# All 22 tiles of gate and up as seven products, with the first two products of 16 tiles computed early and kept in DRAM

## The chip, the cores and the metric

The kernel runs on one core of a Trainium2 chip. The time is that of the device for one execution, in microseconds. Before the change it is 1148.82 us, the median of three runs (1148.8 to 1149.24). The engines are named as in the profile: PE is TensorE, DVE is VectorE, ACT is ScalarE, POOL is GpSimd, SP is SyncE, which issues most DMAs.

## The reference, cut to what matters

One decoder layer on a sequence of 1024 rows of 1024 floats: a norm, attention over windows and a state-space scan in parallel, an output projection, a second norm, and a gated feed-forward network of width 2816. The change touches the part from the scan on.

```python
x = x + gate1 * hybrid_mixer(h, ...)              # attention and scan, then @ w_o
h = rmsnorm(x, norm2) * (1.0 + scale2) + shift2   # the second norm
gu = h @ w_gate_up                                # 1024 x 1024 by 1024 x 5632
g, u = gu[..., :D_FF], gu[..., D_FF:]
x = x + gate2 * ((silu(g) * u) @ w_down)
```

All of it is float32 in and out. Each float32 operand is split into a high and a low part, and a product is three matmuls (`mm3`, L93: high by high, high by low, low by high).

## The kernel before

Gate and up have 22 tiles (`NF`) of 128 columns each. The 1024 rows are two halves of 512, and the 1024 inner rows are eight k-tiles of 128. `h2[half][kt]` is the result of the second norm, transposed and split.

A tile can be done in two ways. In the plain one (`gate_up`, L725), gate and up of one half are eight k-steps of `mm3` each: 48 matmuls for a half, 96 for both. In the other one (`gate_up7`, L881), a two-by-two block scheme after Winograd treats gate and up, the two halves of the inner rows and the two halves of the sequence as blocks, and needs seven products of four k-steps instead of eight: 84 matmuls. The products take sums of the weights' blocks (`w_operand`, L856: four sums on DVE, and for each product a split, which is a cast on ACT and a subtraction on DVE) and sums of h2's blocks (`h2_sums`, L839). Product 0 is the upper half of the gate's weights by the first four k-tiles of h2 of the first half, product 1 the lower half by the last four; their sum is the gate of the first half. Products 2, 3, 4 and 6 take the sums of h2, product 5 takes h2 of the second half, and they need both halves.

Tiles 0 to 3 (`early = 4`) are done the plain way. Their first halves fill PE while the scan's last four chunks (`ssd_chunk`, L573) and the second half's norm wait for other engines; their second halves follow the second half's norm, and cover the time in which the sums of h2 are made. Tiles 4 to 21 are done in seven products. After every pair of tiles `act_sums` (L818) makes four sums on POOL for the seven products of the down projection, and stores seven blocks to DRAM; `dn_weight` (L806) does the like for a block of w_down, in 11 of the tiles (from tile 9 on).

The program is written in one order; a planner lists the instructions of each engine from it, by their order in the program and the time at which it reckons them ready, so instructions of later lines stand between earlier ones. Each engine runs its own list in order. DMAs of SP (`dma`, L71) keep the program's order: SP is a queue in which each DMA waits for the one ahead. ACT issues a few DMAs itself.

Memory: raw weights pass through a ring of three slots (`raw_ring`), split ones through `ws_ring` and, for the seven products, `w_ring` of ten slots. PSUM has four banks tagged "mm" and four tagged "sm". The pools FA and FB hold everything up to the second norm; after it they are closed (L785), and GR and GF are opened in the same memory. `store` (L743) notes a store to DRAM, and `flush` (L746) issues those noted.

Of the kernel before, what the change touches and what calls it, by code (L numbers as in the profile page):

```python
# [15 lines left out]
P = 128  # L16
D = 1024
KT = 8
NF = 22
XNB = ((0, 4, 36, 40), (0, 4, 36, 40))  # L20
# [12 lines left out]
FP_MISC = 1536  # L33
FR_N, FP_N, FA_N, FB_N = 109 * 256, FP_MISC + 3072, 70 * 256 + 8, 6480
GR_N, GF_N, GD_N = 44 * 256, 50 * 256, 92 * 256
# [3 lines left out]
def hymba_layer(ctx: ExitStack, tc: tile.TileContext, x, ada01, ada_rest, w_qk, w_vz, w_xbc,  # L39
# [662 lines left out]
    def second_norm(half, xr, ss):  # L702
        xn = []
        for t in range(4):
            s1 = ring([1], "ss1", 4)
            add(s1, ss[t][:, 0:1], ss[t][:, 1:2])
            r = rstd_of(s1, D, f"r2_{half}{t}", 1)
            n = xn_buf[half][t]
            for e in range(2):
                es = slice(512 * e, 512 * e + 512)  # L710
                nc.vector.tensor_scalar(out=n[:, es], in0=xr[t][:, es], scalar1=r, scalar2=None, op0=ALU.mult)
            dma(x1_d[4 * half + t], xr[t])
            xn.append(n)
        hf_ring = Ring([(FA, 66.03125), (FA, 68.03125)] + ([(FA, 10), (FA, 12)], [(FA, 32), (FA, 34)])[half])
        for kt in range(KT):
            hf = hf_ring([512])
            h_tile(h2[half][kt], xn, kt, g2, sh2, hf, f"h2{half}_{kt}", sm_bank, nc.vector.tensor_copy)
            nc.scalar.dma_start(h2_d[half][kt], hf)
# [4 lines left out]
    early = 4  # L723

    def gate_up(f, half, out, then=None):  # L725
        pss = []
        for s in range(2):
            if (f, s) not in resident:
                resident[(f, s)] = load_w(w_gu[f + NF * s], [KT, P])
            h, l = resident[(f, s)]  # L730
            ps = mm_bank(f"psgu{f}{s}{half}")
            for kt in range(KT):
                t = h2[half][kt]
                mm3(ps, h[:, kt], l[:, kt], t[:, 0], t[:, 1], kt == 0, kt == KT - 1)
            pss.append(ps)
            if then:
                then(s)
        nc.scalar.activation(out, pss[0], AF.Silu)
        mul(out, out, pss[1])
# [41 lines left out]
    for _ in range(3):  # L781
        fetch()
    second_norm(1, xr, ss)
    flush()
# [5 lines left out]
    u_ring, c11, u4 = ring_at(GF, 6, 2, 2), view(GF, 10, [512]), view(GF, 12, [512])  # L790
    pair_ring = ring_at(GF, 14, 8, 2)
    s_act = [view(GF, 30 + 2 * k, [512]) for k in range(3)]
    w_pair = view(GF, 36, [4, 512])
    t_pair = [view(GF, 44 + 2 * k, [512]) for k in range(3)]
# [23 lines left out]
    def act_sums(i, a):  # L818
# [6 lines left out]
        for j, v in (("a11", a11), ("a12", a12), ("a22", a22), ("s1", s1), ("s2", s2), ("s3", a21), ("s4", s4)):  # L825
            if 2 * i >= early or j not in ("a11", "a12"):
                store(act_d, j, i, v)
# [5 lines left out]
    h2_set = [[view(GF, kb + 2 * k, [512]) for k in range(6)] for kb in (36, 0)]  # L833
# [11 lines left out]
    resident = dict(pre)  # L845

    def early_load(n):
        if n < len(order):
            hl = ws_ring([2, D])
            h, l = (hl[:, j].rearrange("p (a b) -> p a b", a=KT) for j in range(2))  # L850
            split(h, l, fetched.pop(order[n]))
            resident[order[n]] = h, l
            fetch()


    def w_operand(n):  # L856
        f, j = divmod(n, 7)
        f += early
        if f >= NF:
            return  # L860
        g, u = fetched[f, 0], fetched[f, 1]
        a11, a12, a21, a22 = g[:, 0:4], g[:, 4:8], u[:, 0:4], u[:, 4:8]
        if j == 2:
            add(s1_w, a21, a22)
            sub(s2_w, s1_w, a11)
        elif j == 4:
            sub(s3_w, a11, a21)
        elif j == 5:
            sub(s2_w, a12, s2_w)
        v = (a11, a12, s2_w, s1_w, s3_w, s2_w, a22)[j]  # L870
        w = w_ring([2, 4, P])
        split(w[:, 0], w[:, 1], v)
        w_ops[n] = w
        if j > 4:
            fetch()

    w_ops = {}
    AHEAD = 5
    rhs = (h2[0][0:4], h2[0][4:8], op_t2, op_t1, op_t3, h2[1][4:8], op_t4)

    def gate_up7(f, out0, out1):  # L881
        u = u_ring([512])
        for j in range(7):
            n = 7 * (f - early) + j
            w_operand(n + AHEAD)
            w, ps = w_ops.pop(n), (mm_bank, sm_bank)[n % 2](f"psg7_{j}_{f}")
# [269 lines left out]
```

## Time and profile before

| | before |
|---|---|
| median of three runs | 1148.82 us |
| profiled execution | 1144.76 us, span 1143.0 us |
| PE, PEld busy | 97%, 80% |
| DVE, ACT, POOL busy | 74%, 45%, 21% |
| mean granted clock of PE | 0.987 |
| DMA | 197.29 MB, 173 GB/s over the span |

The profile is of one execution. Times in it count from the start of its span; the execution takes 1.76 us more than the span. Busy PE counts the time in which a matmul is anywhere in the pipeline, and matmuls overlap, so the pace is read from the starts of many. A bracket behind a row of the timeline is idle time of the engine ahead of that instruction, and what ended it.

### The profile page before, as it was taken

Reading aid. Unit: us, or ns where it says so; the run is one execution under the profiler, and the core shown is the slowest. Engines: PE = TensorE matmul, PEld = TensorE weight load, DVE = VectorE, ACT = ScalarE, POOL = GpSimd, SP = SyncE. Lnnn points to the kernel's source line nnn. Section 1 sums busy time; section 2 is a strip of 40 time slices with the busy share of each in tenths; the row PEclk is TensorE's granted clock in tenths of the full one; section 3 lists DMA queues with packets and bytes.
Section 4 is the critical chain, followed back from the end, with each engine's and each line's share of the span. In section 5 each row is a group of like instructions: output and inputs, shape, how many; then the busy total and the mean of one; then the engine's idle time right before and its main releaser. Section 6 shows DMA issues by size and latency. Waiting matters only on the chain. (4 is left out here: it accounts for less than half of the span.)

```text
span 1143.0 us, 15497 instructions
## 1 busy us (share of the span) xinstructions
PE 1105.0 (97%) x5376; PEld 912.4 (80%) x5376; DVE 842.6 (74%) x1490; ACT 517.2 (45%) x1007; POOL 244.6 (21%) x185
## 2 busy tenths in 40 slices
PE   7999999999999889999999999999999999999996
PEld 6788987787788668887888888888888878888875
DVE  6895368788856466546888888898788648787856
ACT  4573256756565456535443333333333325555431
POOL 0100000001200111000222124554445010451352
PEclk9999999999999969999999999999999999999998
DMA  7555644421320253236753247556764468788733
GB/s 267 189 173 174 238 151 145 137 74 38 148 75 19 102 185 119 76 127 221 249 189 125 67 148 263 194 179 217 256 201 160 157 226 306 252 292 281 234 104 147
DMA packets 80449, 197.29 MB, mean 173 GB/s; under 512 B 9154, under 2 KB 10226, under 8 KB 80244
## 3 DMA queue, kind: packets, MB, share of 16 engines
q1 hardware_dynamic: 74164, 184.95, 47.4%
q10 hardware_dynamic: 6208, 11.37, 2.8%
q8 instruction: 42, 0.69, 0.2%
q14 instruction: 35, 0.29, 0.1%
HBM read 149.87 MB, written 47.98 MB: 173 GB/s over the span
## 5 line engine op out<-in xcount | busy, mean ns | idle before, releaser
L81 DVE TENSOR_TENSOR FR<-FP,FR 128x512 fp32r<-128x512 f32 (+4 forms) x244 | 195.0, 822 | 68.8 <-ACT FR L90 68.3
L90 ACT CAST FR<-FP 128x512 fp32r<-128x512 f32 (+3 forms) x236 | 157.7, 682 | 185.6 <-PE psg L95 79.8
L797 POOL TENSOR_TENSOR GF<-GF 128x512 f32<-128x512 f32 x77 | 124.0, 1633 | 68.9 <-DMA GF<-in_w_dn 65.8
L94 PE MATMUL psg<-FR 128*128 128x512 f32 x306 | 119.0, 389 | 0.0
L95 PE MATMUL psg<-FR 128*128 128x512 f32 x306 | 119.0, 389 | 0.0
L96 PE MATMUL psg<-FR 128*128 128x512 f32 x306 | 119.0, 389 | 0.0
L146 POOL TENSOR_TENSOR FP<-FP 128x1 f32<-128x1 f32 (+1 forms) x40 | 28.3, 713 | 407.8 <-DVE FP L145 351.6
L87 DVE TENSOR_TENSOR GF<-GF,psg 128x512 f32<-128x512 f32 x126 | 84.2, 680 | 30.4 <-PE psg L96 27.9
L90 ACT CAST FR<-GF 128x512 fp32r<-128x512 f32 x77 | 47.4, 619 | 79.8 <-PE psg L95 54.5
L94 PE MATMUL psg<-GR,FR 128*128 128x512 f32 x198 | 77.0, 389 | 0.0
L95 PE MATMUL psg<-GR,FR 128*128 128x512 f32 x198 | 77.0, 389 | 0.0
L96 PE MATMUL psg<-GR,FR 128*128 128x512 f32 x198 | 77.0, 389 | 0.0
L81 DVE TENSOR_TENSOR FR<-GF,FR 128x512 fp32r<-128x512 f32 x77 | 73.1, 951 | 0.9 <-ACT FR L90 0.7
L95 PEld LDWEIGHTS psg<-FR 128*128 128x128 f32 x306 | 57.4, 188 | 12.0
L94 PEld LDWEIGHTS psg<-FR 128*128 128x128 f32 x306 | 57.4, 188 | 11.9
L96 PEld LDWEIGHTS psg<-FR 128*128 128x128 f32 x306 | 57.4, 188 | 11.9
L803 POOL TENSOR_TENSOR GD<-GD 128x512 f32<-128x512 f32 x23 | 35.7, 1562 | 119.7 <-ACT GD L415 57.7
L800 POOL TENSOR_TENSOR GF<-GF 128x512 f32<-128x512 f32 x11 | 15.5, 1405 | 194.3 <-DVE GF L84 156.2
L94 PE MATMUL psgu<-FR 128*128 128x512 f32 x128 | 51.6, 407 | 2.5 <-DVE FR L179 1.3
L94 PE MATMUL psx<-FR 128*128 128x512 f32 x128 | 52.2, 408 | 0.0
L96 PE MATMUL psgu<-FR 128*128 128x512 f32 x128 | 51.4, 403 | 0.5 <-DVE FR L81 0.5
L95 PE MATMUL psx<-FR 128*128 128x512 f32 x128 | 51.8, 405 | 0.0
(318 smaller groups left out, 2748.6 us busy)
## 6 DMA issues: line engine op xcount, KB each, us to landing
FP<-in_w_gu SPq DMA_DIRECT2D x52, 512.0 KB, 4.2
FP<-in_ada_rest SPq DMA_DIRECT2D x24, 512.0 KB, 4.4
actds<-GF SPq DMA_DIRECT2D x44, 256.0 KB, 2.7
GF<-in_w_dn SPq DMA_DIRECT2D x22, 512.0 KB, 4.6
wdndt<-GF SPq DMA_DIRECT2D x44, 256.0 KB, 4.4
FP<-actds SPq DMA_DIRECT2D x44, 256.0 KB, 4.4
FP<-wdndt SPq DMA_DIRECT2D x44, 256.0 KB, 4.4
FP<-actda SPq DMA_DIRECT2D x33, 256.0 KB, 4.2
```

The costliest lines, as they stand in the source:

```text
L81: nc.vector.tensor_tensor(out=out, in0=a, in1=b, op=ALU.subtract)
L87: nc.vector.tensor_tensor(out=out, in0=a, in1=b, op=ALU.add)
L90: nc.scalar.copy(h, raw)
L94: nc.tensor.matmul(ps, lhsT=lh, rhs=rh, start=first, stop=False)
L95: nc.tensor.matmul(ps, lhsT=lh, rhs=rl, start=False, stop=False)
L96: nc.tensor.matmul(ps, lhsT=ll, rhs=rh, start=False, stop=last)
L146: nc.gpsimd.tensor_tensor(out=r, in0=r, in1=mhalf[:, 0:count], op=ALU.pow)
L797: nc.gpsimd.tensor_tensor(out=out, in0=a, in1=b, op=ALU.subtract)
L800: nc.gpsimd.tensor_tensor(out=out, in0=a, in1=b, op=ALU.add)
L803: nc.gpsimd.tensor_tensor(out=out, in0=a, in1=b, op=ALU.mult)
```

## The change

Tiles 0 to 3 are done in seven products too. Of tiles 0 to 15 the first two products need h2 of the first half alone, so they are done early: those of tiles 0 to 7 where the first halves of tiles 0 to 3 were (`first_two`; six before the second half's output projection and two behind it), those of tiles 8 to 15 behind the second half's norm, where the second halves of tiles 0 to 3 were. Product 0, and silu of the sum of both, are stored to DRAM for each of these tiles (`store_uc`, issued by ACT) and loaded again (`load_uc`, on SP) one tile ahead of use. Then tiles 0 to 15 run with five products, and tiles 16 to 21 with seven.

With it go: h2 of the second half is split for the last four k-tiles only; in `h2_sums` two of the four subtractions move from DVE to POOL; operands of the weights are asked for six products ahead instead of five; `dn_weight` moves two tiles later; buffers move in FA, FP and GF.

```diff
-XNB = ((0, 4, 36, 40), (0, 4, 36, 40))
+XNB = ((0, 4, 36, 40), (0, 4, 56.03125, 60.03125))
-FP_MISC = 1536
+FP_MISC = 1440
-GR_N, GF_N, GD_N = 44 * 256, 50 * 256, 92 * 256
+GR_N, GF_N, GD_N = 44 * 256, 52 * 256, 92 * 256
@@ second_norm
-            h_tile(h2[half][kt], xn, kt, ...)
+            h_tile(None if half and kt < 4 else h2[half][kt], xn, kt, ...)
@@
-    early = 4
-    def gate_up(f, half, out, then=None):
...
+    uc_d = {f: DR.tile([P, D], F32, ...) for f in range(16)}
+    BEFORE, FIRST = 8, 16
+    def store_uc(f, uc):
+        nc.scalar.dma_start(uc_d[f], uc.rearrange("p a b -> p (a b)"))
@@
+    uc_early = Ring([(FA, 10), (FA, 36), (FA, 40)])
+    def first_two(f):
+        h, l = load_w(w_gu[f], [KT, P])
+        uc = uc_early([2, 512])
+        for half in range(2):
+            ps = mm_bank(f"psg7_{half}_{f}")
+            for k in range(4):
+                kt = 4 * half + k
+                t = h2[0][kt]
+                mm3(ps, h[:, kt], l[:, kt], t[:, 0], t[:, 1], k == 0, k == 3)
+            if half == 0:
+                nc.scalar.copy(uc[:, 0], ps)
+            else:
+                add(uc[:, 1], uc[:, 0], ps)
+                nc.scalar.activation(uc[:, 1], uc[:, 1], AF.Silu)
+        store_uc(f, uc)
@@
-    for f in range(early - 1):
-        early_gate_up(f)
+    for f in range(BEFORE - 2):
+        first_two(f)
     xr, ss = out_proj(1)
-    flush()
-    early_gate_up(early - 1)
-    pre = {(f, s): load_w(...) for f, s in ((0, 0), (0, 1), (1, 0))}
+    for f in range(BEFORE - 2, BEFORE):
+        first_two(f)
+    wanted = [(f, 0) for f in range(BEFORE, FIRST)] + [(f, s) for f in range(NF) for s in range(2)]
@@
+    w_ring = Ring(free[:2] + [(FR, 16 + 4 * k) for k in range(4)] + free[2:])
+    AHEAD = 6
...
+    for n in range(AHEAD):
+        w_operand(n)
     second_norm(1, xr, ss)
@@
-    u_ring, c11, u4 = ring_at(GF, 6, 2, 2), view(GF, 10, [512]), view(GF, 12, [512])
+    uc_ring, u4 = ring_at(GF, 6, 4, 2), view(GF, 14, [512])
+    pair_ring, uc_first = ring_at(GF, 16, 8, 2), ring_at(GF, 16, 4, 4)
@@ h2_sums
-        for o, v, a, b in ((op_t1, t1, b12, b11), (op_t2, t2, b22, t1), (op_t3, b12, b22, b12), (op_t4, b21, b21, t2)):
-            sub(v, a, b)
+        sub(t1, b12, b11)
+        sub(t2, b22, t1)
+        gsub(b12, b22, b12)
+        gsub(b21, b21, t2)
+        for o, v in ((op_t2, t2), (op_t1, t1), (op_t3, b12), (op_t4, b21)):
             split(o[k][:, 0], o[k][:, 1], v)
@@ gate_up7
+            if j == 3:
+                load_uc(f + 1)
@@
     h2_load(0)
     h2_load(1)
+    for f in range(BEFORE, FIRST):
+        k = f - BEFORE
+        if k < 4:
+            h2_sums(k)
+            if k < 2:
+                h2_load(k + 2)
+        uc = uc_first([2, 512])
+        gate_up7(f, (0, 1), uc)
+        store_uc(f, uc)
+    flush()
+    load_uc(0)
     for i in range(NP):
...
-            if f < early:
-                dma(a[:, r], act_d["a12" if r else "a11", i])
-                h2_sums(f)
...
-                gate_up(f, 1, a[:, 2 + r], lambda s: early_then(f, s))
+            if f < FIRST:
+                gate_up7(f, range(2, 7), ucs.pop(f), a[:, r], a[:, 2 + r])
             else:
-                gate_up7(f, a[:, r], a[:, 2 + r])
+                gate_up7(f, range(7), uc_ring([2, 512]), a[:, r], a[:, 2 + r])
             flush()
-            if 0 <= f - 9 < NP:
-                dn_weight(f - 9)
+            if 0 <= f - 11 < NP:
+                dn_weight(f - 11)
```

## Rows read from the trace of the kernel before

**Rows 1.** The page's line of engines: busy us (share of the span), instructions.
```profile
PE 1105.0 (97%) x5376; PEld 912.4 (80%) x5376; DVE 842.6 (74%) x1490; ACT 517.2 (45%) x1007; POOL 244.6 (21%) x185
```
**Rows 2.** The largest wait of PE over the span: us in total, times, longest.
```profile
PE ps_h L185 <- DVE FA L711: 4.3, 3, 2.5
```
**Rows 3.** Timeline of PE: start, us; transposes, first product, first of down.
```profile
526.14 3.07 PE L185 MATMUL ps_h<-FP,FA 128*128 128x128 f32 x24
...
576.75 0.39 PE L94 MATMUL psg<-FR 128*128 128x512 f32 x1
...
919.47 0.39 PE L94 MATMUL dna<-FR 128*128 128x512 f32 x1
```
**Rows 4.** Groups of PE by line: the first of each three alike.
```profile
L94 PE MATMUL psg<-FR 128*128 128x512 f32 x306 | 119.0, 389 | 0.0
L94 PE MATMUL psg<-GR,FR 128*128 128x512 f32 x198 | 77.0, 389 | 0.0
L94 PE MATMUL psgu<-FR 128*128 128x512 f32 x128 | 51.6, 407 | 2.5 <-DVE FR L179 1.3 <-ACT FR L90 1.1
```
**Rows 5.** Stages: us, busy PE, PEld, DVE, ACT, POOL, clock, DMA, GB/s.
```profile
576.75:652.95 76.20, 76.20 (x338) 63.10 (x337) 64.20 (x96) 27.80 (x50) 13.09 (x9) 1.00 0.38 125
691.05:881.55 190.50, 190.50 (x842) 157.76 (x841) 164.75 (x200) 60.17 (x101) 94.23 (x60) 1.00 0.62 212
419.00:469.40 50.40, 50.40 (x245) 40.68 (x243) 29.32 (x43) 31.44 (x57) 6.26 (x7) 0.96 0.36 125
526.10:576.80 50.70, 48.84 (x226) 38.85 (x225) 40.79 (x58) 24.02 (x35) 7.11 (x4) 1.00 0.76 270
...
544.20:582.20 38.00, 37.48 (x166) 30.71 (x165) 34.65 (x48) 19.87 (x32) 7.11 (x4) 1.00 0.69 242
```
**Rows 6.** SP's queue: a wait, then its timeline at four places.
```profile
SPq L72 <- DMA h2d<-FA: 7.6, 1, 7.6
...
544.24 3.64 SPq L72 DMA_DIRECT2D GF<-h2d  x8
...
862.78 0.84 SPq L72 DMA_DIRECT2D GF<-in_w_dn  x2
...
869.02 4.42 SPq L72 DMA_DIRECT2D wdndt<-GF  x4
...
921.17 0.80 SPq L72 DMA_DIRECT2D actda<-GF  x2
```
**Rows 7.** Timeline of ACT: scan, norm, seven products.
```profile
403.12 1.00 ACTq L718 DMA_DIRECT2D h2d<-FA  x2
...
427.75 1.28 ACT L738 ACT_TABLE_LOAD   x1
429.04 0.60 ACT L738 ACTIVATE FA<-psgu 128x512 f32<-128x512 f32 x1
...
539.11 0.78 ACT L191 ACTIVATE FA<-ps_h,FP 128x512 f32<-128x512 f32 x1 [1.07 <-DMA h2d<-FA]
...
723.65 0.62 ACT L90 CAST FR<-FP 128x512 fp32r<-128x512 f32 x1 [2.10 <-PE psg L95]
```
**Rows 8.** Timelines of POOL and DVE beside each other.
```profile
730.13 5.04 POOL L797 TENSOR_TENSOR GF<-GF 128x512 f32<-128x512 f32 x3
...
733.94 1.78 DVE L81 TENSOR_TENSOR FR<-GF,FR 128x512 fp32r<-128x512 f32 x1
735.65 0.67 DVE L87 TENSOR_TENSOR GF<-GF,psg 128x512 f32<-128x512 f32 x1
736.25 0.68 DVE L81 TENSOR_TENSOR FR<-GF,FR 128x512 fp32r<-128x512 f32 x1
```
**Rows 9.** Timeline of DVE: first sum of a tile's weights, twice.
```profile
589.51 1.20 DVE L87 TENSOR_TENSOR GF<-FP 128x512 f32<-128x512 f32 x1 [2.99 <-DMA FP<-in_w_gu]
...
599.04 0.69 DVE L87 TENSOR_TENSOR GF<-FP 128x512 f32<-128x512 f32 x1
```
**Rows 10.** The page's DMA issues: count, KB each, us to landing.
```profile
FP<-in_w_gu SPq DMA_DIRECT2D x52, 512.0 KB, 4.2
```

More of the change, by code (lines that the diff above doesn't have):

```diff
@@ L716, in second_norm @@
             hf = hf_ring([512])
-            h_tile(h2[half][kt], xn, kt, g2, sh2, hf, f"h2{half}_{kt}", sm_bank, nc.vector.tensor_copy)
+            h_tile(None if half and kt < 4 else h2[half][kt], xn, kt, g2, sh2, hf, f"h2{half}_{kt}", sm_bank, nc.vector.tensor_copy)
             nc.scalar.dma_start(h2_d[half][kt], hf)
@@ L722, in hymba_layer @@
     wdn_d = {(j, i): DR.tile([P, 512], F32, tag=f"wdnd{j}_{i}", name=f"wdnd{j}_{i}") for j in ("t1", "t2", "t3", "t4") for i in range(NP)}
-    early = 4
-    def gate_up(f, half, out, then=None):
[L726 to L739, printed above, removed]
+    uc_d = {f: DR.tile([P, D], F32, tag=f"ucd{f}", name=f"ucd{f}") for f in range(16)}
+    BEFORE, FIRST = 8, 16
+    def store_uc(f, uc):
+        nc.scalar.dma_start(uc_d[f], uc.rearrange("p a b -> p (a b)"))
     stores = []
@@ L782, in hymba_layer, with w_operand @@
         fetch()
+    plan = [(f, j) for f in range(BEFORE, FIRST) for j in range(2)] + [(f, j) for f in range(FIRST) for j in range(2, 7)] + [(f, j) for f in range(FIRST, NF) for j in range(7)]
+    free = [(FR, ws_ring.slots[(ws_ring.i + d) % 3][1] + e) for d in range(3) for e in (0, 4)]
+    w_ring = Ring(free[:2] + [(FR, 16 + 4 * k) for k in range(4)] + free[2:])
+    w_ops = {}
+    AHEAD = 6
+    def w_operand(n):
+        if n >= len(plan):
+            return
+        f, j = plan[n]
+        g, u = fetched[f, 0], fetched.get((f, 1))
+        a11, a12 = g[:, 0:4], g[:, 4:8]
+        if u:
+            a21, a22 = u[:, 0:4], u[:, 4:8]
+        if j == 2:
+            add(s1_w, a21, a22)
+            sub(s2_w, s1_w, a11)
+        elif j == 4:
+            sub(s3_w, a11, a21)
+        elif j == 5:
+            sub(s2_w, a12, s2_w)
+        v = a11 if j == 0 else a12 if j == 1 else a22 if j == 6 else (s2_w, s1_w, s3_w, s2_w)[j - 2]
+        w = w_ring([2, 4, P])
+        split(w[:, 0], w[:, 1], v)
+        w_ops[n] = w
+        if j > 4 or j == 1 and n < 2 * (FIRST - BEFORE):
+            fetch()
+    for n in range(AHEAD):
+        w_operand(n)
     second_norm(1, xr, ss)
-    flush()
     p_f1.close()
@@ L789, in hymba_layer @@
     s1_w, s2_w, s3_w = (view(GF, 2 * k, [4, P]) for k in range(3))
-    u_ring, c11, u4 = ring_at(GF, 6, 2, 2), view(GF, 10, [512]), view(GF, 12, [512])
[L791 to L794, printed above, removed]
+    uc_ring, u4 = ring_at(GF, 6, 4, 2), view(GF, 14, [512])
+    pair_ring, uc_first = ring_at(GF, 16, 8, 2), ring_at(GF, 16, 4, 4)
+    s_act = [view(GF, 32 + 2 * k, [512]) for k in range(3)]
+    w_pair = view(GF, 38, [4, 512])
+    t_pair = [view(GF, 46 + 2 * k, [512]) for k in range(3)]
     def gsub(out, a, b):
@@ L825, in act_sums @@
         for j, v in (("a11", a11), ("a12", a12), ("a22", a22), ("s1", s1), ("s2", s2), ("s3", a21), ("s4", s4)):
-            if 2 * i >= early or j not in ("a11", "a12"):
-                store(act_d, j, i, v)
+            store(act_d, j, i, v)
     op_t1 = [view(FR, 48 + 4 * k, [2, 512]) for k in range(4)]
@@ L832, in hymba_layer @@
     op_t2, op_t3, op_t4 = gr_t[0:4], gr_t[4:8], gr_t[8:12]
-    h2_set = [[view(GF, kb + 2 * k, [512]) for k in range(6)] for kb in (36, 0)]
+    h2_set = [[view(GF, kb + 2 * k, [512]) for k in range(6)] for kb in (38, 0)]
     def h2_load(k):
@@ L840, in h2_sums, with load_uc, gate_up7 @@
         b11, b12, b21, b22, t1, t2 = h2_set[k % 2]
[L841 to L884 removed]
+        sub(t1, b12, b11)
[3 more added lines that the diff above has]
+        for o, v in ((op_t2, t2), (op_t1, t1), (op_t3, b12), (op_t4, b21)):
+            split(o[k][:, 0], o[k][:, 1], v)
+    rhs = (h2[0][0:4], h2[0][4:8], op_t2, op_t1, op_t3, h2[1][4:8], op_t4)
+    ucs = {}
+    def load_uc(f):
+        if f < FIRST:
+            ucs[f] = uc_ring([2, 512])
+            dma(ucs[f].rearrange("p a b -> p (a b)"), uc_d[f])
+    at = [0]
+    def gate_up7(f, js, uc, out0=None, out1=None):
+        u, c11 = uc[:, 0], uc[:, 1]
+        for j in js:
+            n = at[0]
+            at[0] += 1
             w_operand(n + AHEAD)
+            if j == 3:
+                load_uc(f + 1)
             w, ps = w_ops.pop(n), (mm_bank, sm_bank)[n % 2](f"psg7_{j}_{f}")
```

25 lines of the change are left out of this document (3 added, 22 removed).

## The prediction

> **What bounds the kernel now.** I read the engines' line of the page first: TensorE is busy 1105.0 of 1143.0 us, DVE comes next with 74% [rows 1]. Busy is not the same as well used, so the second view is TensorE's waits: the largest of the whole span is 4.3 us in three times [rows 2]. The third is TensorE's timeline over the seven-product tiles: it issues from 576.75 to 919.47 us without one bracket of idle time, and 18 tiles of 84 matmuls are 1512 matmuls [rows 3, 4]. So one matmul of 512 columns costs (919.47 - 576.75) / 1512 = 0.2267 us of the path. (The 389 ns of a group's line are the length of one in the pipeline; they overlap.) The granted clock there is 1.00, that is 2.4 GHz [rows 5]. What shortens TensorE's list is therefore worth its full length, unless another engine then can't keep up; the table of stages says who might: DVE has 164.75 of 190.50 us in the ten tiles from 691 us on, and the DMA engines 0.76 of the stage around the second half's norm [rows 5].
>
> **What is removed.** Before, tiles 0 to 3 cost 96 matmuls each (16 k-steps of three, for two halves), in all 384, and the other 18 cost 84: 384 + 1512 = 1896 (128 x 3, and 306 x 3 + 198 x 3) [rows 4]. After, 22 tiles cost 84: 1848. That is 48 fewer, 48 x 0.2267 = 10.9 us off TensorE's list. Where they stand matters too. Before the second half's norm nothing changes in number: 4 x 48 = 192 matmuls before, 8 tiles x 24 = 192 after. Right behind the norm there are 192 again (4 x 48; now tiles 8 to 15 x 24). The 48 go from the long stage: 1512 before, 16 x 60 + 6 x 84 = 1464 after. The loads of gate and up stay at 52.
>
> **The stage around the second half's norm.** It takes 50.70 us (526.1 to 576.8) [rows 5]. Needed are 192 x 0.2267 = 43.5 us and 32 transposes; the first 24 took 3.07 us [rows 3], so about 3.6 in all: 47.1. So 3.6 us are lost, since the old matmuls there take their right side from h2 of the second half, which comes late: waits on the DVE cast at L179, 1.3 us of it, and slower issue between [rows 4]. The new ones read h2 of the first half alone, which is long there. That loss can go: -3.6. Three things can put a new one in its place.
> (a) Their results go to GF, and GF takes the memory of FA and FB. Its first user before, the load of h2, waits 7.6 us for the store of h2 out of FA and starts at 544.24 [rows 6]. Until then the products may only fill PSUM: four "mm" banks are free, the four "sm" banks belong to the transposes until ScalarE has read them; it does so at 539.11 us for the last, having waited for the h2 stores [rows 7]. Eight products are 8 x 2.72 = 21.8 us, enough to reach 544 if the planner puts the "mm" ones first, and short by the time to the first "sm" bank if it doesn't. I take 1 us; bounds 0 and 7 (from 526.14 with 3.07 us of transposes and one product of 2.72 to the last read at 539.11).
> (b) The sums of h2 must be done when the third product of tile 0 begins, at 526.1 + 47.1 = 573 us if nothing stalls (before: 576.75 + 2 x 2.72 = 582). From 544.2 to 582.2 DVE was busy 34.65 of 38.00 us [rows 5], so this is tight already. After, between 544.2 and 573, DVE has 24 instructions for the sums (8 subtractions go to GpSimd), 8 adds of the new products, 7 splits and 2 sums of weights: 41 x 0.606 = 24.8 us, plus 0.463 for each us of the 8 GpSimd subtractions (12.8 us, by 94.23 / 60 each): 5.9. Sum 30.7 in 29. (0.606 and 0.463 solve two rows: 96 instructions and 13.09 us of GpSimd make 64.20 us, 200 and 94.23 make 164.75 [rows 5].) I take 2 us of stall. Bounds: 0, as three of the four sets are due later; 11.8, if the 8 stores of 512 KB that are new in the stage go ahead of the loads of h2, at 270 / 0.76 = 355 GB/s [rows 5].
> (c) The splits of h2 of the second half for kt below 4 go: 8 DVE instructions, off the path; nothing.
> Stage: -3.6 + 1 + 2, near -0.5; from -3.6 to +12.
>
> **The scan.** Six tiles of 24 matmuls stand where three of 48 stood. TensorE is busy all of 419 to 469.4 us there, ScalarE 31.44 of 50.40 [rows 5]. Added on ScalarE: six copies and three Silu of 0.6 (5.4 us), six store issues (the h2 stores took about 0.5 each, 1.00 for two) and up to three more pairs of table loads, 1.28 us each, as a Silu between the chunks' Exp takes one before and one behind it [rows 7]: 7.7. Up to 16 us on 31, just under the 50. I take +0.5; bounds 0 and 6. In the row the Silu starts 0.01 us after its table load ends (427.75 + 1.28, 429.04). The Trainium skill (ScalarE: Activation LUTs, What ACT_TABLE_LOAD costs) has 1283 ns too, but adds a drain of 1380 ns to every switch. By that, three pairs were 16 us and ScalarE full; the row shows no drain between load and Silu, and I go by the row.
>
> **Tiles 0 to 15 with five products.** TensorE needs 60 x 0.2267 = 13.6 us a tile, DVE does 17 of the 20 instructions (two splits and one add fewer). A pair of tiles with its act_sums on GpSimd (4 x 1.57 = 6.3 us): 34 x 0.606 + 0.463 x 6.3 = 23.5 us of DVE in 27.2: enough. In tiles 11 to 15 dn_weight joins (GpSimd 94.23 / 5 = 18.8 us a pair): 20.6 + 8.7 = 29.3 in 27.2. That is 2.1 a pair short, 5.3 us over five tiles; tiles 16 to 21 (33 in 38.1, 164.75 / 5) give it back. What hides it is the lead of the weights' operands: ScalarE's cast of an operand waits only for TensorE to free its slot (2.10 us at 723.65) [rows 7], and with ten slots that is a lead of about nine products, 24 us. Its price without the lead: 5.3 us. The DMA engines: a pair moves 4 x 512 KB of gate and up, 2 of the kept products, 4 of w_dn, 8 x 256 KB of its sums and 7 of act, 9.2 MB in 27.2 us, 337 GB/s; the row with 0.62 at 212 GB/s would be full at 342 [rows 5]. So both are at their edge for 68 us. I take +2; bounds 0 and 12.
> Beside GpSimd's subtractions (730.13 to 735.17) a DVE instruction with both inputs in SBUF takes 1.78 us, one that reads PSUM 0.67 [rows 8]. The Trainium skill (SBUF - State Buffer, SBUF: two separate sides) calls this an exclusive lock: whichever starts first blocks the other for its whole length. By that, each of the 12 GpSimd instructions of a pair can hold DVE up once, by 1.78 - 0.68 = 1.1: 20.6 + 13.2 = 33.8 us, 16.5 short over five tiles instead of 5.3, still under a full lead of 24. It is the strongest rule against this change; the fitted row says that fewer of them collide.
>
> **The end of the stage.** dn_weight moves from f - 9 to f - 11, so its last two meet tiles 20 and 21. On SP its loads (862.78) are followed by its stores from 869.02 [rows 6]: 6.2 us later. In tile 21 that is long before 921.17, when SP issued the last act sums' stores, which it has to before it opens the next memory. Four more stores stand in that queue, ready by then; nothing, bounds 0 and +3 (four issues).
>
> **The sum.** -10.9 - 0.5 + 0.5 + 2 + 0 = -8.9. The profiled execution took 1144.76 us (1143.0 and what lies around it); 1144.76 - 8.9 = 1135.9. The median of the runs shown is 1148.82, 4.1 higher, and I take the difference from there: 1139.9, called 1140.
>
> **The rivals.**
> - Full saving, 10% : the three losses don't come. 1148.8 - 10.9 - 3.6 = 1134.3. For it: a planner orders the products, and the operand lead covers all. Against: (b).
> - The sums of h2 come late, 8%: the kept products' stores go first on the DMA engines, tile 0 waits 11.8 us at its third product. 1139.9 + 11.8 - 2 = 1150, no change that can be told. For it: 0.76 and 270 GB/s before anything is added. Against: the first two loads are issued at 544, before any such store.
> - The transposes hold the "sm" banks, and products go strictly in turn, 8%: (a) at its upper end, 1139.9 + 7 = 1147, hardly faster. Then the change doesn't do what it says: the products don't run during the norm.
> - Slower, 10%: the weights' raw ring. It has three slots; the second half of the next tile's weights is loaded only when the last sum of this tile has read its slot. Uncontended, from one tile's first sum to the next it is 9.53 us (589.51 to 599.04), 4.2 of it the load [rows 9, 10]. In tiles 11 to 15 GpSimd works 18.8 of 27.2 us, so one of its ten DVE instructions takes 0.31 x 0.68 + 0.69 x 1.78 = 1.44, the loop 4.2 + 14.4 = 18.6 against 13.6: 5.0 x 5 = 25 us less the lead. With no lead the time is 1139.9 - 2 + 25 = 1163; it is slower than before from a lead of under about 14 us (five products) on. For it: tiles 0 to 10 begin with DVE behind (b). Against: in those eleven tiles DVE gains 3.7 us a pair, some 20 in all.
> The forecast has the other 64%, with 1136 to 1144.
>
> **How the numbers follow.** About 0.2%, 1146.5 to 1151.1, is what a measurement of this kernel can't tell from no change. Faster: 64 + 10 + most of the 8 of the banks, 0.80. Same: 0.10. Slower: 0.10. The range reaches from just under the full saving to the late sums, 1133.5 to 1150; the slower case is outside.
>
> **What would show it.** TensorE with 48 matmuls fewer and the same pitch of 0.2267. No wait on L179 in the norm's stage; "psg" products between the transposes. If (b) holds, a wait of one to three us for a DVE split ahead of tile 0's third product. In tiles 11 to 15 DVE near 0.95 or more and TensorE without waits; if waits for DVE splits or for w_gu stand there, the raw ring decides, and the time is above 1150. A gap before "dna" of over 2 us would make the end wrong.

## The result: slower, 1165.0 us, and the profile after

| | before | after |
|---|---|---|
| median of four runs | 1148.81 us | 1165.00 us (1164.42 to 1168.11) |
| ratio, 95% interval | | 1.0149 [1.0128, 1.0169] |
| profiled execution, span | 1144.76, 1143.0 | 1164.56, 1162.7 |

The prediction was 1140 with a range up to 1150. From the page of after, the engines [rows 1] and the loads of gate and up [rows 10]:

```profile
PE 1107.6 (95%) x5328; PEld 905.5 (78%) x5328; DVE 864.2 (74%) x1522; ACT 512.8 (44%) x1015; POOL 257.4 (22%) x193
...
FP<-in_w_gu SPq DMA_DIRECT2D x60, 512.0 KB, 5.0
```

TensorE has the 48 matmuls less (5376 to 5328), and is yet busy longer. TensorE's timeline of after at the places of [rows 3]: the transposes, the third product of tile 0, the first two of down. (`psg` are the PSUM banks of gate and up, `dna` to `dng` those of the seven down products.)

```profile
527.93 2.35 PE L185 MATMUL ps_h<-FP,FA 128*128 128x128 f32 x20
...
580.58 0.40 PE L94 MATMUL psg<-GR,FR 128*128 128x512 f32 x1
...
927.88 0.49 PE L94 MATMUL dna<-FR 128*128 128x512 f32 x1 [1.59 <-ACT FR L90]
930.16 0.80 PE L95 MATMUL dna<-FR 128*128 128x512 f32 x1 [1.79 <-DVE FR L81]
```

These starts cut the span in four, for this kernel and for each one below (us; the third column is what the prediction expected of the change):

| stage | before | expected | after | uc_late | dn9 | uc_late + dn9 | all3 | all3_nosub |
|---|---|---|---|---|---|---|---|---|
| start to transposes | 526.1 | +0.5 | 527.9 | 530.3 | 528.9 | 530.5 | 526.7 | 525.8 |
| norm, first two products | 50.6 | -0.5 | 52.6 | 52.3 | 52.3 | 53.9 | 52.3 | 53.5 |
| tiles | 342.7 | -8.9 | 347.3 | 337.5 | 343.4 | 337.5 | 338.7 | 331.8 |
| down, to the end | 223.5 | 0 | 234.8 | 237.0 | 230.9 | 230.2 | 232.2 | 223.4 |

Each column is one profiled execution, and those of one kernel differ by some us (all3's lie between 1148.16 and 1155.32). One execution of all3_ahead5 was slow, 1224.59 us at a granted clock of 0.844; it is left out of that kernel's time, and since it is the one that was profiled, its stages are not given.

After is 19.7 us longer in these profiles: 1.8 + 2.0 + 4.6 + 11.3. The tiles should have taken 1464 x 0.2267 = 331.9 us and took 15.4 more. TensorE's largest waits from 519 to 960 us (us in total, times, longest):

```profile
PE dna L94 <- DVE GF L87: 3.9, 2, 2.2
PE psg L94 <- ACT FR L90: 3.4, 3, 1.9
PE psg L96 <- DVE FR L81: 3.1, 4, 1.1
PE dna L94 <- ACT FR L90: 2.6, 2, 1.6
```

In the tiles, up to the first of down, TensorE stops six times for 6.5 us in all, and 3.2 us more are lost in slower steps right behind these stops. The rest, 5.7 us, is in the pitch, the time from one matmul's start to the next, of matmuls that do not wait. It was 0.2310 us in the five-product tiles and 0.2298 in the others, against 0.2267 before.

**SP's queue in the tiles.** The first fence is SP's largest wait between 580 and 770 us (us in total, times, longest), the second SP's timeline, the third DVE's.

```profile
SPq L72 <- DVE GF L84: 120.6, 12, 16.6
```
```profile
645.77 0.33 SPq L72 DMA_DIRECT2D GF<-ucd  x1
...
659.39 0.32 SPq L72 DMA_DIRECT2D GF<-ucd  x1
659.76 0.90 SPq L72 DMA_DIRECT2D FP<-in_w_gu  x2
```
```profile
656.27 0.69 DVE L81 TENSOR_TENSOR GF<-FP,GF 128x512 f32<-128x512 f32 x1
...
658.68 0.69 DVE L84 TENSOR_TENSOR GF<-GF 128x512 f32<-128x512 f32 x1
659.28 0.69 DVE L81 TENSOR_TENSOR FR<-FP,FR 128x512 fp32r<-128x512 f32 x1
...
664.18 0.69 DVE L87 TENSOR_TENSOR GF<-FP 128x512 f32<-128x512 f32 x1 [2.83 <-DMA FP<-in_w_gu]
```

The kept sums have two slots. The load for the next tile (`GF<-ucd`) stands at product 3 in SP's queue and waits until DVE's last multiplication of the tile before (L84, 658.68) has freed its slot. It goes at 659.39, and right behind it go two loads of gate and up. The first of them needed no such wait: DVE read its slot for the last time at 656.27. (The second had to wait for the split at 659.28 in any case.) DVE waits for the first (664.18), and its own next multiplication stands behind that in its list. So there is a loop: it turns in 13.3 to 15.9 us, 14.5 in the mean of tiles 3 to 13, where TensorE needs 13.6 at the old pitch.

The loop eats up the lead, the time from a tile's first sum of weights on DVE to its third product on TensorE. Before, it was 28 to 37 us from the fourth seven-product tile on. After, it falls from 15.8 us in tile 3 to 9.0 in tile 13 and 3.9 in tile 14 (771.69 to 775.55), and there TensorE begins to wait.

**The end.** SP's queue, DVE's list, and the row of a part of the stretch (busy PE, PEld, DVE, ACT, POOL, clock, DMA, GB/s):

```profile
914.25 4.53 SPq L72 DMA_DIRECT2D wdndt<-GF  x4
919.97 0.81 SPq L72 DMA_DIRECT2D GF<-in_w_dn  x2
...
921.30 0.42 SPq L72 DMA_DIRECT2D FP<-actda  x1
```
```profile
927.24 1.19 DVE L81 TENSOR_TENSOR FR<-FP,FR 128x512 fp32r<-128x512 f32 x1 [12.46 <-ACT FR L90]
928.36 0.68 DVE L87 TENSOR_TENSOR GF<-GF,psg 128x512 f32<-128x512 f32 x1
```
```profile
930.20:942.20 12.00, 8.09 (x17) 5.44 (x18) 10.41 (x16) 4.06 (x8) 2.49 (x2) 0.50 0.46 160
```

The last load of w_down (919.97) and four stores that waited for POOL (914.25 on) stand ahead of the first operands of down (921.30). DVE's list has the split of such an operand at its head (927.24, idle 12.46 us), with the additions behind it that empty PSUM for tile 21 (928.36 on). So TensorE starts down 1.6 us late and stops four more times, for 1.79, 1.70, 2.21 and 0.97 us. After the first two of these stops its granted clock falls: it is 0.50, the lower level of 1.2 GHz, from 930.2 to 942.2 us, where matmuls that don't wait are 0.43 us apart. dna takes 41.8 us instead of 31.3. Of these 10.5 us, 5.6 are longer stops (6.67 against 1.06); most of the others are the lower clock. dnb to dng are as before within 1 us.

### The profile page after: what moved, and what is told of

Its sections match the earlier page's. It is cut to its first block, busy times and chain, and to the rows that moved or that the text cites. A ratio compares the mean times of both kernels' runs of the same rounds, so it can differ in the third digit from the quotient of the medians.

```text
span 1162.7 us, 15435 instructions
## 1 busy us (share of the span) xinstructions
PE 1107.6 (95%) x5328; PEld 905.5 (78%) x5328; DVE 864.2 (74%) x1522; ACT 512.8 (44%) x1015; POOL 257.4 (22%) x193
## 5 line engine op out<-in xcount | busy, mean ns | idle before, releaser
L81 DVE TENSOR_TENSOR FR<-FP,FR 128x512 fp32r<-128x512 f32 (+4 forms) x232 | 193.2, 860 | 63.3 <-ACT FR L90 62.6
L90 ACT CAST FR<-FP 128x512 fp32r<-128x512 f32 (+3 forms) x224 | 144.2, 668 | 95.3 <-DMA FP<-actda 40.9
L825 POOL TENSOR_TENSOR GF<-GF 128x512 f32<-128x512 f32 x85 | 135.9, 1620 | 120.5 <-DMA GF<-in_w_dn 81.0
L94 PE MATMUL psg<-FR 128*128 128x512 f32 x374 | 148.7, 398 | 5.3 <-ACT FR L90 2.6
L96 PE MATMUL psg<-FR 128*128 128x512 f32 x374 | 148.5, 397 | 1.7 <-DVE FR L81 1.7
L95 PE MATMUL psg<-FR 128*128 128x512 f32 x374 | 148.1, 396 | 0.0
L90 ACT CAST FR<-GF 128x512 fp32r<-128x512 f32 x93 | 56.7, 619 | 161.5 <-DVE GF L87 108.8
L87 DVE TENSOR_TENSOR GF<-GF,psg 128x512 f32<-128x512 f32 x146 | 97.2, 680 | 6.0 <-DMA GF<-ucd 2.5
L94 PE MATMUL psg<-GR,FR 128*128 128x512 f32 x242 | 95.6, 395 | 1.5 <-ACT FR L90 1.5
L96 PE MATMUL psg<-GR,FR 128*128 128x512 f32 x242 | 95.8, 396 | 1.3 <-DVE FR L81 1.3
L95 PE MATMUL psg<-GR,FR 128*128 128x512 f32 x242 | 95.1, 393 | 0.0
L94 PEld LDWEIGHTS psg<-FR 128*128 128x128 f32 x374 | 71.1, 190 | 22.5 <-ACT FR L90 3.7
L96 PEld LDWEIGHTS psg<-FR 128*128 128x128 f32 x374 | 71.0, 190 | 18.3 <-DVE FR L81 2.9
L95 PEld LDWEIGHTS psg<-FR 128*128 128x128 f32 x374 | 71.3, 191 | 15.4
L81 DVE TENSOR_TENSOR FR<-GF,FR 128x512 fp32r<-128x512 f32 x93 | 81.9, 892 | 0.3 <-ACT FR L90 0.2
L96 PEld LDWEIGHTS psg<-GR,FR 128*128 128x128 f32 x242 | 45.4, 188 | 12.9 <-DVE FR L81 2.2
L94 PEld LDWEIGHTS psg<-GR,FR 128*128 128x128 f32 x242 | 45.4, 188 | 12.7 <-ACT FR L90 2.4
L95 PEld LDWEIGHTS psg<-GR,FR 128*128 128x128 f32 x242 | 45.5, 188 | 10.5
L94 PE MATMUL psx<-FR 128*128 128x512 f32 x128 | 52.6, 411 | 0.0
```

What stands on the lines that cost most here:

```text
L81: nc.vector.tensor_tensor(out=out, in0=a, in1=b, op=ALU.subtract)
L87: nc.vector.tensor_tensor(out=out, in0=a, in1=b, op=ALU.add)
L90: nc.scalar.copy(h, raw)
L94: nc.tensor.matmul(ps, lhsT=lh, rhs=rh, start=first, stop=False)
L95: nc.tensor.matmul(ps, lhsT=lh, rhs=rl, start=False, stop=False)
L96: nc.tensor.matmul(ps, lhsT=ll, rhs=rh, start=False, stop=last)
```

## The experiments

Every kernel ran on the same chip as before did beside it, not all on one chip; the ratios are to the time of before there, 1147.58 to 1148.04 us. The expectations from all3_nosub on cut all3 in another way: they give its tiles as 339.6 us and its down part, up to the last matmul, as 222.9. The table above has 338.7 and, up to the end of the span, 232.2.

**Load of the kept sums (uc_late).**
```diff
-            if j == 3:
+            if j == 6:
                 load_uc(f + 1)
```


> The changed kernel with one edit: the load of the kept products of the next tile stands at the seventh product of a tile instead of the fourth, so behind the two loads of weights that stood behind it in SP's queue. Theory L (a loop): in the changed kernel DVE's last multiplication of a tile frees the slot, SP then loads the kept products, only then the weights, and DVE waits for these; the loop takes some 14.7 us a tile against 13.6 of TensorE, so the lead of the operands falls from 15.8 to 3.9 us. By L one more tile of slack comes back: leads of 20 us and more in tiles 4 to 15, no waits of TensorE from 580 to the end of the seven products, pitch near 0.2267 again, the stage from the third product of tile 0 to the first down product 333 to 337 us instead of 347; time 1147 to 1155, as the end of the stage stays. Rival C (DVE beside GpSimd is too slow in tiles 11 to 15, whatever the queue): leads still fall below 6 us at tile 14, time 1162 to 1165.

1157.01, ratio 1.0084 [1.0048, 1.0120]; L's range ended at 1155. SP's and DVE's waits in the same stretch as above, against 120.6 for L84, and against 26.9 for DVE in after:

```profile
SPq L72 <- DVE GF L81: 66.4, 9, 12.8
SPq L72 <- DVE FR L81: 56.2, 14, 8.8
SPq L72 <- DVE GF L84: 7.8, 11, 1.3
```
```profile
DVE GF L87 <- DMA FP<-in_w_gu: 12.2, 12, 3.5
```

SP waits about as long as in after, but now mostly for DVE's reads of the weights' own slots (L81). The lead is 16 to 27 us from tile 3 on, TensorE has no stop in the tiles, and they take 337.5. The loop cost 9.8 us of tiles. The pitch stayed 0.2310, against L's 0.2267, and 337.5 - 331.9 = 5.6 us is what that costs. The end is not touched (dna 41.2).

**Down weights (dn9, uc_late_dn9, before_dn11).** f - 9 in after, alone and with the last edit; f - 11 in before.
```diff
-            if 0 <= f - 11 < NP:
-                dn_weight(f - 11)
+            if 0 <= f - 9 < NP:
+                dn_weight(f - 9)
```


> The changed kernel with the blocks of w_down back at tiles 9 to 19 (f - 9). Theory E (the end): the last two blocks' loads on SP, 908 and 920 us, wait for each other's stores and hold the first operands of the down projection back to 921; by E the first of these loads goes out some 15 us earlier, the down part takes 224 to 227 us again instead of 235, and the time is 1153 to 1158, the tiles being the same or up to 4 us worse. Rival (the end is only late because DVE's list has no lead): the down part stays above 231 us, time 1163 to 1168.

> Both edits. L and E together: 1137 to 1143, below the kernel before. If C holds instead of L: 1153 to 1158. If the end needs only the lead: the same as the kernel with the late load alone.

> The kernel before with the blocks of w_down at f - 11. By E the end costs here too, though the operands have their full lead of 28 to 36 us: the down part 230 us or more instead of 223.5, time 1154 to 1160. By the rival (only the lead matters), and by the step of the prediction that priced it at 0 to 3: 1148 to 1152.

dn9: 1157.75, 1.0086 [1.0052, 1.0119]. Both: 1152.96, 1.0049 [1.0023, 1.0076]. before_dn11: 1151.54, 1.0037 [1.0009, 1.0065]. The late place costs a little before, too: its tiles are the same 342.7, its end 229.8 instead of 223.5 in the profile. Of these 6.3 us, 2.8 are in dna; 3.4 are in dnf, which is between 31.0 and 35.3 us long among all these profiles. The time lies in the rival's range. Moving the blocks back takes 3.9 us off the end in after, not 11.3: dna still takes 36.9. So dn9 has the time that E forecast, but not its down part of 224 to 227. The two repairs give 12.0 us together and missed their expectation, so something else was left.

**The pitch (before_1440, after_1408).** FP_MISC is the first part of FP; what lies behind it, FP's rings and the pools GR and GF, moves with it. By the sizes GR starts at 254 x 512 bytes in before, 384 bytes lower in after, and at 253 x 512 with 1408.
```diff
-FP_MISC = 1536
+FP_MISC = 1440
```


> The kernel before with FP_MISC = 1440 instead of 1536 and nothing else: GR begins 384 bytes earlier, 128 bytes past a multiple of 512. Theory A: its matmuls psg<-GR go from 0.2267 to 0.2323 us, those of tiles 4 to 21 (18 tiles of 4 products of 12, 864, or with tile sums kept in FR fewer), so TensorE's work grows by 4 to 6 us and the time is 1152 to 1155. Rival B: nothing changes, 1148.

> The changed kernel with FP_MISC = 1408 instead of 1440: the operand block GR, which lies behind FP, begins at a multiple of 512 bytes of each partition again, as it did before the change; nothing else is moved. Theory A (the base address of the moving operand sets the pitch): matmuls psg<-GR go from 0.2323 back to 0.2267 us, some 1460 of them by 0.0056 to 0.007, so TensorE's own work in the tiles falls by 5 to 8 us. As DVE's loop and the late down weights still set the pace of much of the stage, the time falls by 1 to 6 us, to 1159 to 1164. Rival B (the pitch is slower because more operands are taken from GR, or because five products a tile switch more often): the pitch stays at 0.2323 and the time at 1165.

Timeline of TensorE, first and twelfth matmul of one product from GR; before_1440, then after_1408:

```profile
622.74 0.40 PE L94 MATMUL psg<-GR,FR 128*128 128x512 f32 x1
...
625.30 0.39 PE L96 MATMUL psg<-GR,FR 128*128 128x512 f32 x1
```
```profile
622.90 0.39 PE L94 MATMUL psg<-GR,FR 128*128 128x512 f32 x1
...
625.40 0.39 PE L96 MATMUL psg<-GR,FR 128*128 128x512 f32 x1
```

2.56 us against 2.50 for eleven steps (2.49 in before, 2.54 to 2.56 in after). This one number makes the kernel before slower: 1153.22, 1.0044 [1.0025, 1.0063], its tiles 347.3 instead of 342.7. With 1408 the pitch of after is 0.2270 where TensorE doesn't wait, and yet nothing is gained that can be told: 1162.33, 1.0123 [1.0076, 1.0170], its tiles 347.4 in a profile of its slowest run, 1168.23. There SP waits as long as ever, so the loop sets the pace:

```profile
SPq L72 <- DVE GF L84: 118.8, 12, 15.2
```

**The three together (all3), and with them h2's sums on DVE again, in the order of before (all3_h2, the last seven lines).**
```diff
-FP_MISC = 1440
+FP_MISC = 1408
...
-            if j == 3:
+            if j == 6:
...
-            if 0 <= f - 11 < NP:
-                dn_weight(f - 11)
+            if 0 <= f - 9 < NP:
+                dn_weight(f - 9)
...
-        sub(t1, b12, b11)
-        sub(t2, b22, t1)
-        gsub(b12, b22, b12)
-        gsub(b21, b21, t2)
-        for o, v in ((op_t2, t2), (op_t1, t1), (op_t3, b12), (op_t4, b21)):
+        for o, v, a, b in ((op_t1, t1, b12, b11), (op_t2, t2, b22, t1), (op_t3, b12, b22, b12), (op_t4, b21, b21, t2)):
+            sub(v, a, b)
```


> The changed kernel with three things put right: kept sums loaded at a tile's last product (j = 6 instead of 3), down weights begun at f - 9 instead of f - 11, and FP_MISC = 1408. The first two alone gave 1153.0. Theory A with the two others: 5 to 8 us less, 1145 to 1148, which is about the kernel before. If the pitch has nothing to do with the base address: 1153.

> The same three, and the sums of h2 all on DVE in the order of the kernel before (two of four were moved to POOL). Theory: the sums' operands were late by 1.9 us (567 us) in the changed kernel because POOL holds DVE's port while it subtracts; with them on DVE the stretch from the 192nd to the 384th matmul falls from 52.5 to 51 us, 1 to 2 us of the whole. Rival: DVE's list is then longer by 8 subtractions of 0.68 us in the same tiles, and the wait stays or grows by up to 3 us.

all3: 1149.83, 1.0021 [0.9999, 1.0044], above its expectation of 1145 to 1148. all3_h2: 1150.21, 1.0027 [1.0005, 1.0049]; its norm stage is 55.5 instead of 52.3, its tiles 334.3 instead of 338.7. Two subtractions on POOL are not what costs there. all3 has TensorE's full pitch and its tiles are still no shorter than with uc_late at the slow pitch: another engine is the bound.

**dn_weight's subtractions left out (all3_nosub, before_nosub).**
```diff
-        gsub(t1, b12, b11)
-        gsub(t2, b22, t1)
-        gsub(b12, b22, b12)
-        gsub(t4, b21, t2)
-        for j, v in (("t1", t1), ("t2", t2), ("t3", b12), ("t4", t4)):
+        for j, v in (("t1", b11), ("t2", b22), ("t3", b12), ("t4", b21)):
```


> The changed kernel with the three repairs (kept sums at j = 6, down weights from f - 9, FP_MISC = 1408; 1149.8 us, tiles 339.6, down part 222.9), and dn_weight's four subtractions on POOL left out: it stores the raw blocks of w_down instead of their sums, so loads and stores are the same and only POOL's work goes. Theory P (what is left of the loss comes from those subtractions: they hold DVE's port, and SP's queue waits for them, L825 67 us between 600 and 920, with the loads of w_gu behind): tiles 333 to 335 and the down part 216 to 219, 1138 to 1144 in all. Rival Q (DVE's own list, 17 instructions in 13.6 us, and the waits of the stores' DMA are the limit): 1147 to 1150.

> The kernel before, with dn_weight's four subtractions left out, as in the run that took 13.6 us off the repaired kernel. Theory (before, a lead of some 30 us hides them): no change, 1146 to 1149. Rival (they cost there as well): 1135 to 1142.

all3_nosub: 1136.27, 0.9902 [0.9868, 0.9936]. before_nosub: 1146.98, 0.9997 [0.9980, 1.0015]. The same 44 subtractions cost 13.6 us in the repaired kernel and nothing in the one before. (Without them the stores no longer wait for POOL, so this is what POOL's work and SP's wait for it cost together.) TensorE's waits from 576 to 960 us, all3 and then all3_nosub, whole:

```profile
PE psg L94 <- DVE GF L87: 4.1, 3, 2.2
PE dna L94 <- DVE GF L87: 2.6, 1, 2.6
PE dna L94 <- ACT FR L90: 1.7, 1, 1.7
PE psg L96 <- DVE FR L81: 1.3, 2, 1.1
```
```profile
PE dna L94 <- ACT FR L90: 0.8, 1, 0.8
```

The stretch 745 to 800 us, columns as in [rows 5], of before, all3 and all3_nosub:

```profile
745.00:800.00 55.00, 55.00 (x244) 45.55 (x243) 49.31 (x61) 17.67 (x30) 27.11 (x18) 1.00 0.58 200
```
```profile
745.00:800.00 55.00, 52.59 (x229) 42.17 (x227) 48.95 (x54) 11.70 (x20) 35.26 (x22) 1.00 0.70 246
```
```profile
745.00:800.00 55.00, 55.00 (x244) 45.57 (x243) 46.89 (x67) 14.46 (x25) 13.09 (x8) 1.00 0.84 298
```

Before, the stretch holds 2.9 tiles; in all3, with shorter tiles, four, so POOL has 35 us of work in it instead of 27. DVE finishes 54 instructions in 48.95 us there, and 67 in 46.89 without the subtractions. Its list in all3 beside a stretch of POOL shows why (POOL, then DVE):

```profile
755.03 11.83 POOL L825 TENSOR_TENSOR GF<-GF 128x512 f32<-128x512 f32 x7
```
```profile
755.42 1.78 DVE L84 TENSOR_TENSOR GF<-GF 128x512 f32<-128x512 f32 x1
757.12 0.67 DVE L87 TENSOR_TENSOR GF<-GF,psg 128x512 f32<-128x512 f32 x1
```

The multiplication, with both inputs in SBUF, takes 1.78 us beside POOL and 0.69 alone (769.48); the addition, which reads PSUM, takes 0.67 beside POOL and 0.68 alone (770.08). The lead, 16 to 22 us in tiles 6 to 12 of all3, falls to 3.9 in tile 15; in all3_nosub it stays above 14 from tile 6 on.

**By which way, and where else (eight kernels on all3).** all3_actq: dn_weight's loads and stores on ACT's queue. all3_ahead9, all3_ahead5: operands asked for 9 or 5 products ahead. all3_dndve: its subtractions on DVE. spread: its eleven units in the tiles of DN_AT.
```diff
-            dma(x[0], x[1])
+            nc.scalar.dma_start(x[0], x[1]) if x[2][0] == "t" else dma(x[0], x[1])
...
-    AHEAD = 6
+    AHEAD = 9
...
-        gsub(t1, b12, b11)
+        sub(t1, b12, b11)
...
+    DN_AT = (3, 5, 7, 9, 11, 13, 15, 16, 17, 18, 19)
...
-            if 0 <= f - 9 < NP:
-                dn_weight(f - 9)
+            if f in DN_AT:
+                dn_weight(DN_AT.index(f))
```


> The three repairs, and the loads of w_dn and the stores of its sums issued by ACT instead of SP; POOL's work is unchanged. Theory S (the queue's order alone: w_gu's loads stand behind stores that wait for POOL): the loads come when their slot is free, tiles 334 to 336, in all 1143 to 1147. If POOL's hold on DVE's port is the cause instead: 1149 to 1151. If ACT's own list is held up by the stores' waits, its casts come late and it is slower than 1151.

> The three repairs, and AHEAD = 9 instead of 6: the operands of the weights are asked for three products earlier, of ten slots. Theory: if the lead is limited by where the program asks, it grows by up to three products (8 us) and the waits in tiles 13 to 16 (about 6 us) go: 1144 to 1147. If the arrival of w_gu limits it (DVE waited 18.7 us for it between 690 and 900), nothing changes: 1149 to 1151.

> Both of the last two edits. If loads and program order limit the lead together, this alone gives the full gain: tiles 332 to 334, 1141 to 1145. Otherwise the better of the two.

> The three repairs, and AHEAD = 5 as in the kernel before. AHEAD = 9 cost 22 us (tiles 352.7 instead of 339.6, down part 230.0 instead of 222.9), as DVE's list then has more splits of later operands ahead of the sums that empty PSUM. Theory O (that cost is about even per step of AHEAD, 7 us): 1142 to 1146. Rival (only past some value do the splits stand in front of what TensorE needs; at 5 the lead is shorter): 1149 to 1153.

> The three repairs, and dn_weight's four subtractions on DVE instead of POOL; nothing is left out. Theory P (POOL's hold of the port costs DVE about as much as doing the work: 0.463 x 1.6 = 0.73 us for each against 0.61, and SP's stores wait 1.6 us a subtraction): a gain of 3 to 8 us, 1142 to 1147. Rival (DVE's list is full and the waits between dependent subtractions stand in it): 1150 to 1156.

> Both: subtractions on DVE and AHEAD = 5. If both theories hold, 1138 to 1143, faster than the kernel before by 0.5 to 0.9%. If neither does, 1150 to 1157.

> The three repairs and the same eleven tiles, with the subtractions on POOL and AHEAD = 6: only the place of the units differs from the repaired kernel of 1149.8. A pair with one unit: 20.6 + 0.463 x (6.3 + 6.4) = 26.5 us in 27.2. Theory: tiles 333 to 336, 1143 to 1147. Rival: 1148 to 1152.

> The three repairs, AHEAD = 5, dn_weight's subtractions on DVE, and its eleven units in tiles 3, 5, 7, 9, 11, 13, 15, 16, 17, 18, 19 instead of 9 to 19. DVE's need by the fit of the kernel before: a pair of five-product tiles with act_sums and one unit 20.6 + 2.9 + 2.4 = 25.9 us in 27.2, so the lead no longer falls. Theory (the place decides): tiles 332.5 to 335, 1141 to 1145, faster than before. Rival (the amount decides, the SP queue waits as long): 1146 to 1150.

| | time | ratio | tiles | down |
|---|---|---|---|---|
| all3_actq | 1175.18 | 1.0233 [1.0198, 1.0267] | 366.5 | 224.0 |
| all3_ahead9 | 1171.61 | 1.0204 [1.0171, 1.0237] | 351.8 | 239.4 |
| all3_actq9 | 1189.56 | 1.0357 [1.0310, 1.0405] | 384.6 | 222.2 |
| all3_ahead5 | 1155.30 | 1.0061 [1.0039, 1.0083] | | |
| all3_dndve | 1151.64 | 1.0038 [1.0018, 1.0058] | 333.8 | 234.3 |
| all3_dndve5 | 1146.82 | 0.9989 [0.9970, 1.0007] | 336.0 | 226.1 |
| spread | 1151.12 | 1.0025 [1.0007, 1.0044] | 340.3 | 233.4 |
| spread_dve5 | 1156.94 | 1.0071 [1.0047, 1.0095] | 340.5 | 229.9 |

all3_actq, all3_dndve and spread came out in a range that was written down, each time not the theory's; the other five came out in none.

On ACT's queue the stores' waits hold up ACT's casts instead (two of ACT's waits from 600 to 920 us that all3 doesn't have):

```profile
ACT FR L90 <- POOL GF L825: 47.1, 10, 8.8
ACT FR L90 <- DMA wdndt<-GF: 28.1, 5, 10.3
```

So that run doesn't separate the queue from DVE's slow instructions. In spread SP waits 24.2 us for L825 instead of 67.0, and the tiles are no shorter, so their price doesn't follow that wait alone. But the queue isn't cleared either. Here is how all3's lead falls to 3.9 in tile 15 (SP, then DVE):

```profile
760.08 7.13 SPq L72 DMA_DIRECT2D wdndt<-GF  x4
...
772.81 0.89 SPq L72 DMA_DIRECT2D FP<-in_w_gu  x2
```
```profile
767.42 0.68 DVE L81 TENSOR_TENSOR GF<-FP,GF 128x512 f32<-128x512 f32 x1
...
779.03 0.82 DVE L87 TENSOR_TENSOR GF<-FP 128x512 f32<-128x512 f32 x1 [5.68 <-DMA FP<-in_w_gu]
```

DVE's last read of the slot is at 767.42. The load stands behind dn_weight's stores, which wait for POOL, and goes at 772.81; DVE then stops 5.68 us for it. What share each way has was not separated. With the subtractions on DVE the tiles are 5 us shorter in that profile, its end is 2 longer, and the median is no better. Asking for operands earlier makes it slower, not faster: dna then takes 44.5 us. Five instead of six is slower with POOL and faster with DVE; why is open.

**What is left of the end.** The store ahead of down's first operand in SP's queue waits for DVE's last multiplication of tile 20 (L84); SP and DVE of before, then of all3:

```profile
902.48 0.38 SPq L72 DMA_DIRECT2D FP<-actda  x1
```
```profile
901.35 0.69 DVE L84 TENSOR_TENSOR GF<-GF 128x512 f32<-128x512 f32 x1
```
```profile
908.54 0.42 SPq L72 DMA_DIRECT2D FP<-actda  x1
```
```profile
907.45 0.69 DVE L84 TENSOR_TENSOR GF<-GF 128x512 f32<-128x512 f32 x1
```

The operand is asked for 17.0 us ahead of dna before and 9.1 us in all3 (6.6 in after). Over all profiles but all3_ahead5's, dna takes 30.3 to 34.1 us where this is 15.9 us or more, and 36.3 to 44.5 where it is 13.3 or less. So what is left of the end goes with DVE's lost lead; no run changes that alone. all3_actq's down part of 224.0 fits this and doesn't clear up more: its tiles are 28 us longer, and the operand is asked for 17.0 us ahead. No version that does all the work beats the kernel before; the best, all3_dndve5, is level with it.

## Why the prediction was wrong, step by step

- **48 matmuls at 0.2267: right.** all3_nosub has its tiles in 331.8 us, against the 331.9 of the working. It is 10.7 us below before_nosub (1136.27, 1146.98), near the 10.9 of the working: that is what the change gives with the three repairs and where dn_weight's subtractions cost nothing, as they do before.
- **"The loads of gate and up stay at 52": wrong.** There are 60: the gate's weights of tiles 0 to 15 are read twice, 16 loads more, where before gate and up of tiles 0 to 3 were, 8 loads more. What the 8 cost was not separated.
- **The norm's stage, -0.5: +2.0, inside its bounds.** The waits on L179 [rows 4] are gone, as expected. The "sm" banks (a) cost one wait of 0.72 us at 537. The sums (b) cost 3.6 instead of 2, and in another place. Tile 0's third product (580.58) does not wait. TensorE stops at 567.25, 569.04 and 575.45, for 1.90, 1.05 and 0.68 us, in the early products of tiles 8 to 15: their weights' casts on ACT and splits on DVE (`FP` is where the raw weights lie) stand behind those of the sums.
```profile
567.25 0.50 PE L94 MATMUL psg<-FR 128*128 128x512 f32 x1 [1.90 <-ACT FR L90]
```
```profile
566.06 0.62 ACT L90 CAST GR<-GF 128x512 fp32r<-128x512 f32 x1 [0.60 <-POOL GF L825]
566.59 1.13 ACT L90 CAST FR<-FP 128x512 fp32r<-128x512 f32 x2
```
- **Two sums of that stage were a little off.** 8 x 94.23 / 60 is 12.6, not 12.8; and at 3.07 us for 24, 32 transposes take 4.1 us, not 3.6, so 3.1 us were lost there before and not 3.6.
- **The scan, +0.5: not resolved.** +1.8 in this profile, but kernels nearly alike up to there lie between 525.3 and 530.9. Of the "up to three more pairs of table loads" none came: seven loads between 380 and 527 us in both kernels, each of 1.28 us, with the activation 0.01 us behind it (429.00 and 430.29 in after). The drain that the Trainium skill adds (ScalarE: Activation LUTs, What ACT_TABLE_LOAD costs) shows in no row here.
- **Five-product tiles, +2: this step failed.** It was +15.4, beyond its bound of 12. "A lead of about nine products, 24 us" was taken from the kernel before, as if the ring's ten slots made it. But a lead has to be built up, and the loop that builds it was new. `load_uc` was counted in the DMA bytes alone; that it takes a place in SP's queue and waits there, with the weights' loads behind it, was left out (9.8 us). The "same pitch of 0.2267" was taken over though buffers moved; the smaller FP_MISC cost 5.7 us (960 x 0.0043 + 504 x 0.0031).
- **DVE with POOL: the sum of 29.3 us in 27.2 was right in kind.** It was called hidden by the lead. With the loop and the pitch repaired it shows: 338.7 - 331.8 = 6.9 us of tiles and 8.8 of the end in these profiles, 13.6 in all by the medians. A DVE instruction takes 0.91 us in the stretch with 35 us of POOL, 0.81 with 27 and 0.70 with 13 (48.95 / 54, 49.31 / 61, 46.89 / 67). The lock of the Trainium skill (SBUF - State Buffer, SBUF: two separate sides), weighed there as the strongest rule against the change, fits that, and the rows at 755.03 to 757.12 above. That DVE is slow beside POOL is shown; that this, and not SP's wait for POOL, makes the 13.6 us is not. The prediction's row for a PSUM reader of 0.67 [rows 8] starts at 735.65, when POOL has already ended at 735.17, so it doesn't show what it was quoted for; the row at 757.12 does.
- **The end of the stage, "nothing, bounds 0 and +3": this step failed too.** It was +11.3. The four issues were counted. That the stores wait for POOL, with down's first operands behind them, that DVE's list then stops on such an operand ahead of tile 21's additions, and that TensorE's granted clock falls to 0.50 after its stops, was not. Putting dn_weight back takes off 3.9 us; the rest goes with DVE's lost lead, as far as the runs show.
- **The slower rival** had the right kind, a loop through SP's queue, and by chance the time, 1163. It was put in the wrong ring (the weights' raw slots) and in tiles 11 to 15 beside POOL; the loop stood in the ring of kept sums in tiles 3 to 13, most of them without dn_weight. More than half of the loss, the end, was no part of it.

## What to carry to other kernels

A load that must wait for a buffer delays every load behind it in its queue: place it in program order where its buffer is free, and price a new DMA by the wait of what stands behind it. A lead seen in an old trace is the product of the old pace; ask whether the new loop can build it before using it as cover. When a size changes, check where every later buffer begins.

## What the runs showed of the hardware that was not expected

A shift of buffers by 384 bytes changed TensorE's pitch. In before_1440 a product whose moving operand lies in GR took 2.56 us for eleven steps and one from FR, which had not moved, 2.51; in before both took 2.49. With 1408 in after they took 2.49 to 2.50. GR starts at a multiple of 512 bytes in both fast cases and not in the slow one; that it is this, and not the shift of DVE's and ACT's buffers in FP and GF beside it, was not separated.
